# Five plain projection blocks, two pieces of fill per attention step, and more places for gates in a one-core decoder layer

## The chip, the cores and the metric

One core of a Trainium2 chip runs the whole layer in one program. The metric is device time in microseconds (us). TensorE does the matrix products into PSUM, VectorE (DVE in the profile) and ScalarE (ACT) read PSUM and SBUF, GpSimd (POOL) works on SBUF alone, and SyncE (SP) issues the DMAs.

## The reference, cut to what matters

The layer takes `x` (1024 tokens by 1024 channels). One projection `p = x @ w_in` feeds four token mixers: A, an RWKV-7 recurrence; B, a causal convolution; C, gated linear attention; D, forgetting attention (a causal softmax attention with a bias from cumulated log forget gates). Each mixer's output `u_b` (256 channels) is projected up to 1024 channels and gated:

```
gates  = sigmoid(p_gate.reshape(T, 4, D) + gate_b)
merged = gates[:, 0] * (u_rw @ rw_up)  + gates[:, 1] * (u_cv @ cv_up) \
       + gates[:, 2] * (u_gla @ gla_up) + gates[:, 3] * (u_fox @ fox_up)
x = layer_norm(ALPHA * x + merged @ w_out)
```

After that come a cross-attention and a SwiGLU network with their own residuals and norms. Everything is in float32.

## The kernel before, in words

A float32 product is made of three matmuls of a rounded type: each operand is split into a high part (a cast on ACT) and a low part (a subtraction, on DVE unless told otherwise) by `split` (lines 161 and 162), and `mm3` adds high*high, low*high and high*low (lines 179, 183, 182). A matmul has 512 columns, one half of the 1024 tokens.

**Projection (from line 407 on).** The weight matrix comes in blocks of 128 output columns. `plain(b)` makes one block: two halves of 8 x 3 matmuls, a copy out of PSUM on ACT, and `shift(b)`, the token shift in five DVE instructions (lines 327 to 331). Blocks 0, 1 and 8 are made so. The other blocks are made in pairs by `seven`, a Strassen-like scheme with 7 products of 4 x 3 matmuls in place of 8; it needs sums and differences of quarters of `x` and of the weights. `sums_of_x0(k)` makes those of `x`: four POOL instructions (`comb` at line 389, and line 449) and three splits into the tiles `xt`. It is called for k = 0 to 3, and each call sets one of the eight `xraw` places of the pool `pM` free, from which the plain blocks' results `praw` and the first weight `piece` take theirs. Block 8's weights (`w_misc`) are asked for just behind block 0.

**Mixers, with fill.** While the recurrence and the attentions run, TensorE's gaps are filled from a generator, `merge` (`pieces` at its call). A piece is six matmuls: a quarter of a half of a gate block (`gate_block`, tile `ps_g`; `ps_gate` for the first branch) or one product of `other_branches` (`ps_up`, a mixer output times `ups`). `weave(fill, streams, n)` draws n pieces and then takes one step of each stream. For forgetting attention n is `FOX_PIECES`, 3. `fox` has 20 steps for each of two head pairs, and `weave` draws once more at its end. `head` is one head and block of 128 queries, in three stages one step apart: scores (`ps_fs`, line 1094 for the mask), with maximum, exponential and normalisation on DVE and ACT; transposes (`ps_ft`, line 1115); output (`ps_fo`, line 1128, after every second one).

`merge` gives 80 pieces of the first branch, and then for j = 0 to 7 the 8 pieces of one of the last branch's gate blocks, followed by up to 4 products of the other branches, or up to 10 once forgetting attention has ended (`3 in ready`). The last branch, 3, can begin only then. `drain(pieces)` takes what is left.

A product of `other_branches` is six matmuls into one of two PSUM banks, a multiplication by the gate on DVE (line 1256), and an addition to `merged` on POOL (line 1257). The gates were stored in DRAM and come back by DMA into tiles `gsig` (line 1245); there are three places for them (tag `sg`), and `ahead` asks for them two products before their use. The outputs of a branch are loaded and split by `values` into `yh` and `yl`, which have room for one branch. After the products `merged` is split (`mA`, `mB`) and multiplied by `w_out`, whose weights take the places of `xh` and `xl` when the last gate block has been made.

**What sets the order.** Each engine's instructions are put in order by a planner at build time. It takes the first instruction in program order that is ready by its own cost estimates, and waits for a free place of the pool, so later work may move ahead of work that waits. On the chip the order of each engine is then fixed.

Of the kernel before, what the change touches and what calls it, by code (L numbers as in the profile page):

```python
# [11 lines left out]
F32 = mybir.dt.float32  # L12
# [4 lines left out]
ALU = mybir.AluOpType  # L17
PSUM = bass.MemoryType.PSUM
INVERSE = 14
FOX_PIECES = 3  # L20
DRAM = bass.MemoryType.DRAM

P = 128
# [3 lines left out]
TH = 512  # L27
# [10 lines left out]
ST_BLOCKS = ["cb0", "ca0", "cb1", "ca1", "gq", "gk", "gv0", "gv1", "gr0", "gr1",  # L38
             "fq0", "fk0", "fv0", "fq1", "fk1", "fv1"]
# [53 lines left out]
def hybrid_kernel(ctx, tc, io, out):  # L93
# [10 lines left out]
    pB = ctx.enter_context(tc.tile_pool(name="pB", bufs=9))  # L104
# [55 lines left out]
    def split(hi, lo, src, eng=nc.vector):  # L160
        nc.scalar.copy(hi, src)  # L161
        eng.tensor_tensor(out=lo, in0=src, in1=hi.bitcast(F32), op=ALU.subtract)  # L162

    def weight(src, pool=wp, th="whi", tl="wlo", eng=nc.vector, rp=wp, tr="raw"):
        raw = rp.tile([P, D], F32, tag=tr, name="wraw")
        nc.sync.dma_start(raw, src)
        hi = pool.tile([P, D], F32R, tag=th, name="whi")
        lo = pool.tile([P, D], F32R, tag=tl, name="wlo")
        split(hi, lo, raw, eng)
        return hi, lo  # L170
# [21 lines left out]
    def drain(gen, n=None):  # L192

        while n is None or n > 0:
            if next(gen, gen) is gen:
                return
            n = n if n is None else n - 1

    def collect(gen, res):
        res.append((yield from gen))  # L200
# [76 lines left out]
    def hs(hf):  # L277
        return slice(hf * TH, (hf + 1) * TH)
# [113 lines left out]
    def sums(raws):  # L392
        a11, a21, a22 = raws[0][:, 0:TH], raws[1][:, 0:TH], raws[1][:, TH:]
        s1 = comb(a21, a22, ALU.add)
        s2 = comb(s1, a11, ALU.subtract)
        return s1, s2, comb(a11, a21, ALU.subtract)

    def plain(bi, w=None, between=None):
        raw = pM.tile([P, T], F32, tag="M", name="praw")
        g = project(io["wblk"][bi], lambda hf, ps: nc.scalar.copy(raw[:, hs(hf)], ps), w)  # L400
        drain(g, 1)
        if between:
            between()
        drain(g)
        shift(bi, raw)

    with ExitStack() as es:
        xtp = es.enter_context(tc.tile_pool(name="xtp", bufs=12))
        pairs0 = list(range(2, 8, 2)) + list(range(9, 9 + len(ST_BLOCKS), 2))

        def rows(u):
            pool, tag = (pM, "M") if u % 2 else (wp, "raw")
            raws = []
            for i in range(2):
                raws.append(pool.tile([P, D], F32, tag=tag, name="wraw"))
                nc.sync.dma_start(raws[i], io["wblk"][pairs0[u] + i])
            return raws

        def making(sv):
            nxt, ss = rows(0), None  # L420
            for u in range(len(pairs0)):
                raws = nxt
                a = [r[:, i * TH:(i + 1) * TH] for r in raws for i in range(2)]
                s1, s2, s3 = ss or sums(raws)
                yield sv.piece(a[0])
                if u + 1 < len(pairs0):
                    nxt = rows(u + 1)
                for src in (a[1], s2, s1, s3, a[3]):
                    yield sv.piece(src)
                t = sv.piece(comb(a[1], s2, ALU.subtract))  # L430
                ss = sums(nxt) if u + 1 < len(pairs0) else None
                yield t

        sv = Sevens(((pM, "M"), (wp, "whi"), (wp, "wlo"), (wp, "whi"), (wp, "wlo")), making)
        plain(0, w_first)

        xt = [tuple([t[:, i] for t in ts for i in range(2)] for ts in
                    ([xtp.tile([P, 2, TH], F32R, tag="xt", name="xt") for _ in range(2)] for _ in range(2)))
              for _ in range(3)]

        def sums_of_x0(k):
            (b11, b12), (b21, b22) = ([xraw[i][:, hs(hf)] for hf in range(2)] for i in (k, k + HK))
            t1 = comb(b12, b11, ALU.subtract)
            split(xt[0][0][k], xt[0][1][k], t1)
            t2 = comb(b22, t1, ALU.subtract)
            split(xt[1][0][k], xt[1][1][k], t2)
            t3 = comb(b22, b12, ALU.subtract)
            split(xt[2][0][k], xt[2][1][k], t3)
            nc.gpsimd.tensor_tensor(out=b11, in0=b21, in1=t2, op=ALU.subtract)

        w_misc = weight(io["wblk"][8])
        for k in (0, 1):
            sums_of_x0(k)
        plain(1, w_second)
        for k in (2, 3):
            sums_of_x0(k)
        plain(8, w_misc, lambda: sv.top_up(3))

        def quarter(i, hf):
            return [t[:, hs(hf)] for t in xh[HK * i:HK * i + HK]], [t[:, hs(hf)] for t in xl[HK * i:HK * i + HK]]  # L460


        x12 = quarter(0, 1)
        for k in range(HK):
            split(x12[0][k], x12[1][k], xraw[k][:, hs(0)])
        rhs0 = (quarter(0, 0), quarter(1, 0), xt[1], xt[0], xt[2], x12, quarter(1, 1))

        def term():
            t = pM.tile([P, 2, TH], F32, tag="M", name="term")
            return t[:, 0], t[:, 1]  # L470

        def bank0():
            return gps("ps_g")

        for b in pairs0[0:3]:
            raws = [pM.tile([P, T], F32, tag="M", name="praw") for _ in range(2)]

            def done(i, l, a, ps):
                tt(out=raws[i][:, hs(l)], in0=a, in1=ps, op=ALU.add)

            sv.seven(rhs0, bank0, term, done)
            for i in range(2):
                shift(b + i, raws[i])
        for b in pairs0[3:]:
            held = {}

            def done(i, l, a, ps):
                n = BLOCKS[b + i]
                t = pM.tile([P, TH], F32, tag="M", name="stg2")
                tt(out=t, in0=a, in1=ps, op=ALU.add)  # L490
                if n[0] == "c":
                    if n[1] == "b":
                        act(t, t, AF.Sigmoid)
                    held.setdefault(l, []).append(t)
                    if len(held[l]) < 2:
                        return
                    tt(out=t, in0=t, in1=held[l][0], op=ALU.mult)
                    n = "cu" + n[2]
                elif n[:2] == "fq":
                    act(t, t, AF.Copy, scale=0.125)  # L500
                nc.sync.dma_start(st_d[n][:, hs(l)], t)

            sv.seven(rhs0, bank0, term, done)
        for k in range(HK):
            t = pM.tile([P, TH], F32, tag="M", name="x12")
            nc.sync.dma_start(t, io["xT"][k][:, hs(1)])
            split(x12[0][k], x12[1][k], t)
# [725 lines left out]
    def other_branches(t2):  # L1233

        for br in (1, 2, 3):
            while br not in ready:
                yield None
            y = values(br, t2)
            us, todo, sgs = [up_weights(br, 0, t2)], [(j, hf) for j in range(KD) for hf in range(2)], []

            def ahead(n):
                while len(sgs) < min(n, len(todo)):
                    j, hf = todo[len(sgs)]
                    t = t2.tile([P, TH], F32, tag="sg", name="gsig", bufs=3)
                    nc.sync.dma_start(t, gate_d[8 * br + j - 8, :, hs(hf)])
                    sgs.append(t)

            ahead(2)
            yield None
            for n, (j, hf) in enumerate(todo):  # L1250
                if hf == 0 and j + 1 < KD:
                    us.append(up_weights(br, j + 1, t2))
                pu = gps("ps_up", both=False)
                up_product(pu, us[j], y, hf)
                sg, mj = sgs[n], merged[j][:, hs(hf)]
                tt(out=sg, in0=sg, in1=pu, op=ALU.mult)  # L1256
                nc.gpsimd.tensor_tensor(out=mj, in0=mj, in1=sg, op=ALU.add)  # L1257
                ahead(n + 3)
                yield True

    def merge(t2):
# [14 lines left out]
    ready = {0}  # L1276
    with ExitStack() as es:
# [13 lines left out]
        with tc.tile_pool(name="t3", bufs=4) as t3:  # L1291
            c_d = []
            weave(pieces, [collect(fox_decay(t3, ps2), c_d)])
            weave(pieces, [fox(t3, ps2, c_d[0])], FOX_PIECES)
        drain(pieces)
# [459 lines left out]
    late = []  # L1755
# [101 lines left out]
    for k in range(HK):  # L1857
        t = diff(x2[k + HK][:, hs(0)], xt[0].h[k + HK].bitcast(F32))
# [78 lines left out]
    for n, sl in enumerate((slice(0, 512), slice(512, 768), slice(768, 1024))):  # L1937
        hf, w = sl.start // TH, sl.stop - sl.start
# [12 lines left out]
        ahead = 3 if n < 2 else 1  # L1951
# [110 lines left out]
```

## Time and profile before

| | |
|---|---|
| median of 3 runs | 2127.74 us (2120.87 to 2127.99) |
| profiled execution | 2121.39 us |
| its span, first to last instruction | 2119.6 us |
| TensorE busy | 2052.0 us (97%), 11392 matmuls |
| mean granted TensorE clock | 0.984 |

The profile is of one execution. In its rows a time is in us from the span's start, and "idle before" is the idle time of that engine ahead of the instruction, with what released it. A matmul's own time overlaps the next one's; the distance between two starts is what one costs.

### The profile page before, as it was taken

How to read it: one execution, taken by the hardware profiler on the slowest of the kernel's cores; microseconds unless marked ns; L12 is line 12 of the kernel's file. 1: busy time of each engine (PE TensorE's matmuls, PEld its weight loads, DVE VectorE, ACT ScalarE, POOL GpSimd, SP SyncE). 2: the span in 40 equal slices, each digit the busy share in tenths (PEclk: the TensorE clock that was granted, in tenths of full speed). 3: DMA queues.
4: the chain of work that ended last, by engine and by line, in shares of the span. 5: the costliest groups of instructions: out<-in, count | busy, mean ns of one | idle time of the engine just before them, and what ended most of it. 6: DMA issues, size and time to landing. Idle time of an engine off the chain costs nothing.

```text
span 2119.6 us, 29300 instructions
## 1 busy us (share of the span) xinstructions
PE 2052.0 (97%) x11392; PEld 1672.8 (79%) x11392; DVE 1305.0 (62%) x2249; ACT 782.4 (37%) x1332; POOL 437.0 (21%) x328
## 2 busy tenths in 40 slices
PE   8999999999999999997899999999999999999997
PEld 5888877877777787775689788877888888888877
DVE  8975465398624544545567445687566666666666
ACT  4332254222257465563134333344232222232331
POOL 5432200000000001214313100047121212222343
PEclk9999999999999999998999999999999999999998
DMA  5223343231222314336434212330311111211112
GB/s 168 70 79 110 105 132 91 68 99 62 75 99 83 89 44 139 106 104 192 136 115 127 75 38 65 105 120 22 118 40 40 66 54 41 70 50 40 54 47 80
DMA packets 100507, 181.09 MB, mean 85 GB/s; under 512 B 21030, under 2 KB 45400, under 8 KB 100368
## 3 DMA queue, kind: packets, MB, share of 16 engines
q1 hardware_dynamic: 100368, 179.21, 26.2%
q8 instruction: 90, 1.47, 0.3%
q14 instruction: 49, 0.40, 0.1%
HBM read 141.84 MB, written 37.34 MB: 85 GB/s over the span
## 4 chain that ended last, share of the span: by engine, by line
PE 84%; DVE 5%; POOL 3%; issue 3%; ACT 3%; DMA 2%; SPq 0%; DVEq 0%; POOLq 0%; ACTq 0%
PE ps_w L183 9%; PE ps_w L179 9%; PE ps_w L182 9%; PE ps_g L179 8%; PE ps_g L183 7%; PE ps_g L182 7%; PE ps_q L182 3%; PE ps_q L183 3%; PE ps_q L179 2%; PE ps_wo L182 1%; PE ps_wo L183 1%; PE ps_wo L179 1%; PE ps_gate L179 1%; PE ps_gate L183 1%; PE ps_gate L182 1%
## 5 line engine op out<-in xcount | busy, mean ns | idle before, releaser
L182 PE MATMUL ps_g<-xh,wlo 128*128 128x512 f32 x432 | 171.7, 397 | 4.1 <-DVE wlo L162 4.1
L183 PE MATMUL ps_g<-xl,whi 128*128 128x512 f32 x432 | 171.9, 398 | 0.0
L161 ACT CAST piece<-wraw 128x512 fp32r<-128x512 f32 x135 | 82.9, 621 | 202.6 <-PE ps_w L183 160.9
L179 PE MATMUL ps_g<-xh,whi 128*128 128x512 f32 x432 | 148.7, 418 | 0.8 <-ACT xh L161 0.8
L161 ACT CAST piece<-wcomb 128x512 fp32r<-128x512 f32 x116 | 70.7, 620 | 212.4 <-PE ps_w L183 133.2
L183 PE MATMUL ps_w<-hid,piece 128*128 128x512 f32 (+1 forms) x400 | 144.3, 368 | 2.4 <-DVE hid L162 2.4
L182 PE MATMUL ps_w<-hid,piece 128*128 128x512 f32 (+1 forms) x400 | 144.0, 367 | 0.0
L162 DVE TENSOR_TENSOR wlo<-wraw,whi 128x1024 fp32r<-128x1024 f32 x77 | 97.7, 1270 | 58.6 <-ACT whi L161 58.3
L389 POOL TENSOR_TENSOR wcomb<-wraw,wcomb 128x512 f32<-128x512 f32 x29 | 42.0, 1448 | 398.8 <-DVE piece L162 397.8
L1781 DVE TENSOR_TENSOR x<-x,ps_w 128x512 f32<-128x512 f32 x120 | 82.4, 687 | 65.4 <-PE ps_w L183 65.3
L162 DVE TENSOR_TENSOR piece<-wraw,piece 128x512 fp32r<-128x512 f32 x127 | 99.1, 783 | 34.8 <-ACT piece L161 31.7
L161 ACT CAST whi<-wraw 128x1024 fp32r<-128x1024 f32 x95 | 98.6, 1046 | 56.0 <-issue 18.4
L162 POOL TENSOR_TENSOR wlo<-wraw,whi 128x1024 fp32r<-128x1024 f32 x18 | 46.1, 2567 | 323.5 <-ACT whi L161 312.7
L183 PE MATMUL ps_w<-xT,piece 128*128 128x512 f32 x288 | 112.0, 389 | 0.0
L182 PE MATMUL ps_w<-xT,piece 128*128 128x512 f32 x288 | 112.0, 389 | 0.0
L179 PE MATMUL ps_w<-hid,piece 128*128 128x512 f32 (+1 forms) x400 | 108.8, 367 | 0.2 <-DVE x L1779 0.2
L389 POOL TENSOR_TENSOR wcomb<-wraw 128x512 f32<-128x512 f32 x60 | 82.6, 1377 | 99.9 <-DVE piece L162 50.3
L182 PEld LDWEIGHTS ps_g<-xh,wlo 128*128 128x128 f32 x432 | 82.3, 191 | 22.9 <-DVE wlo L162 4.6
L1257 POOL TENSOR_TENSOR merged<-merged,gsig 128x512 f32<-128x512 f32 x48 | 69.1, 1452 | 139.3 <-DVE gsig L1256 128.0
L183 PEld LDWEIGHTS ps_g<-xl,whi 128*128 128x128 f32 x432 | 82.4, 191 | 18.6 <-issue 0.8
L162 DVE TENSOR_TENSOR piece<-wcomb,piece 128x512 fp32r<-128x512 f32 x116 | 91.7, 798 | 6.3 <-ACT piece L161 5.6
L179 PEld LDWEIGHTS ps_g<-xh,whi 128*128 128x128 f32 x432 | 76.6, 192 | 22.4 <-issue 4.6
(528 smaller groups left out, 5304.4 us busy)
## 6 DMA issues: line engine op xcount, KB each, us to landing
wraw<-ffn_w SPq DMA_DIRECT2D x72, 512.0 KB, 5.5
wraw<-wblk SPq DMA_DIRECT2D x57, 512.0 KB, 3.6
gate_d<-gsig SPq DMA_DIRECT2D x48, 256.0 KB, 2.0
gsig<-gate_d SPq DMA_DIRECT2D x48, 256.0 KB, 2.9
wraw<-xa_wo SPq DMA_DIRECT2D x16, 512.0 KB, 3.5
xraw<-xT SPq DMA_DIRECT2D x16, 256.0 KB, 5.6
yld<-y_d SPq DMA_DIRECT2D x16, 256.0 KB, 2.6
uraw<-ups SPq DMA_DIRECT2D x32, 128.0 KB, 3.6
```

The costliest lines, as they stand in the source:

```text
L161: nc.scalar.copy(hi, src)
L162: eng.tensor_tensor(out=lo, in0=src, in1=hi.bitcast(F32), op=ALU.subtract)
L179: mm(ps, lhsT=pairs[i][0], rhs=pairs[i][2], start=start and i == 0, stop=False)
L182: mm(ps, lhsT=ll, rhs=rh, start=False, stop=False)
L183: latest[0] = mm(ps, lhsT=lh, rhs=rl, start=False, stop=stop and i == n + min(lag, n) - 1)
L389: nc.gpsimd.tensor_tensor(out=t, in0=a, in1=b, op=op)
L1257: nc.gpsimd.tensor_tensor(out=mj, in0=mj, in1=sg, op=ALU.add)
L1781: tt(out=xs, in0=xs, in1=ps, op=ALU.add)
```

## The change

The pair of blocks 2 and 3 leaves the seven-product scheme, and both are made by `plain`. The calls of `sums_of_x0` are spread: one ahead of each of blocks 1, 2, 3 and 8. `FOX_PIECES` goes from 3 to 2. Once forgetting attention has ended, the gates of `other_branches` take places of the pool `pB` (tag `B`, nine places, shared with attention's tiles before and with `mA` after) in place of the three of `sg`, and are asked for four products ahead in place of two.

```diff
-FOX_PIECES = 3
+FOX_PIECES = 2
...
-        pairs0 = list(range(2, 8, 2)) + list(range(9, 9 + len(ST_BLOCKS), 2))
+        pairs0 = list(range(4, 8, 2)) + list(range(9, 9 + len(ST_BLOCKS), 2))
...
-        w_misc = weight(io["wblk"][8])
-        for k in (0, 1):
-            sums_of_x0(k)
+        w = weight(io["wblk"][2])
+        sums_of_x0(0)
         plain(1, w_second)
-        for k in (2, 3):
-            sums_of_x0(k)
-        plain(8, w_misc, lambda: sv.top_up(3))
+        w, w_next = weight(io["wblk"][3]), w
+        sums_of_x0(1)
+        plain(2, w_next)
+        w, w_next = weight(io["wblk"][8]), w
+        sums_of_x0(2)
+        plain(3, w_next)
+        sums_of_x0(3)
+        plain(8, w, lambda: sv.top_up(3))
...
-        for b in pairs0[0:3]:
+        for b in pairs0[0:2]:
...
-        for b in pairs0[3:]:
+        for b in pairs0[2:]:
...
-                    t = t2.tile([P, TH], F32, tag="sg", name="gsig", bufs=3)
+                    late = 3 in ready
+                    t = (pB if late else t2).tile([P, TH], F32, tag="B" if late else "sg", name="gsig",
+                                                  bufs=9 if late else 3)
...
-                ahead(n + 3)
+                ahead(n + (5 if 3 in ready else 3))
```

## Rows read from the trace of the kernel before

**Rows 1.** The page: busy time by engine; TensorE in 40 slices, tenths.

```profile
PE 2052.0 (97%) x11392; PEld 1672.8 (79%) x11392; DVE 1305.0 (62%) x2249; ACT 782.4 (37%) x1332; POOL 437.0 (21%) x328
...
PE   8999999999999999997899999999999999999997
```

**Rows 2.** Waits of TensorE, 952.5 to 1031 us: total, times, longest.

```profile
PE ps_up L179 <- DVE gsig L1256: 12.0, 12, 2.0
PE ps_up L179 <- ACT yh L161: 8.2, 2, 6.7
PE ps_wo L179 <- ACT mA L161: 1.3, 1, 1.3
```

**Rows 3.** The same view, 19 to 62 us.

```profile
PE ps_g L182 <- DVE wlo L162: 4.1, 1, 4.1
PE ps_g L182 <- DVE piece L162: 3.2, 1, 3.2
PE ps_g L179 <- ACT piece L161: 1.4, 1, 1.4
```

**Rows 4.** Timeline of TensorE at the start: start, duration, count, idle before.

```profile
23.95 0.39 PE L182 MATMUL ps_g<-xh,wlo 128*128 128x512 f32 x1
24.18 0.39 PE L183 MATMUL ps_g<-xl,whi 128*128 128x512 f32 x1
...
35.06 0.80 PE L182 MATMUL ps_g<-xh,wlo 128*128 128x512 f32 x1 [4.14 <-DVE wlo L162]
...
40.72 0.39 PE L183 MATMUL ps_g<-xl,whi 128*128 128x512 f32 x1
...
47.77 0.39 PE L183 MATMUL ps_g<-xl,whi 128*128 128x512 f32 x1
...
60.23 1.07 PE L179 MATMUL ps_g<-xt,piece 128*128 128x512 f32 x4
```

**Rows 5.** Timeline of VectorE and GpSimd in the same stretch.

```profile
30.05 1.60 POOL L449 TENSOR_TENSOR xraw<-xraw,wcomb 128x512 f32<-128x512 f32 x1
...
32.12 1.75 DVE L331 SCALAR_TENSOR_TENSOR r<-r,par,praw 128x512 f32<-128x512 f32 x1
33.79 1.21 DVE L162 TENSOR_TENSOR wlo<-wraw,whi 128x1024 fp32r<-128x1024 f32 x1
...
59.09 0.68 DVE L329 TENSOR_TENSOR misc<-praw 128x512 f32<-128x512 f32 x1
```

**Rows 6.** By stretch: busy us of PE, PEld, DVE, ACT, POOL; granted clock; DMA.

```profile
727.00:952.40 225.40, 222.29 (x1289) 177.80 (x1287) 108.93 (x243) 139.71 (x246) 31.44 (x24) 1.00 0.29 94
```

**Rows 7.** The same view: `ps_up`'s instructions alone (PE, PEld, DVE), then `ps_g`'s.

```profile
952.40:1028.00 75.60, 45.30 (x168) 32.81 (x168) 18.12 (x27) 0.91 0.57 181
...
952.40:1028.00 75.60, 9.81 (x42) 7.80 (x42) 0.00 (x0) 1.38 (x2) 0.91 0.57 181
```

**Rows 8.** Timeline of the last branch's products on VectorE and GpSimd.

```profile
1016.49 2.73 POOL L1257 TENSOR_TENSOR merged<-merged,gsig 128x512 f32<-128x512 f32 x2 [1.29 <-DVE gsig L1256]
...
1016.95 0.69 DVE L1256 TENSOR_TENSOR gsig<-gsig,ps_up 128x512 f32<-128x512 f32 x1 [0.60 <-DMA gsig<-gate_d]
1017.55 0.52 DVE L162 TENSOR_TENSOR ul<-uraw,uh 128x256 fp32r<-128x256 f32 x1
1018.47 1.30 DVE L162 TENSOR_TENSOR mA<-merged,mA 128x512 fp32r<-128x512 f32 x1 [0.40 <-ACT mA L161]
```

**Rows 9.** Timeline of one attention unit, from its masked scores to the normalisation.

```profile
783.61 0.23 PE L1094 MATMUL ps_fs<-lvl,identb 128*128 128x128 bf16 x1
...
784.93 1.28 ACT L1104 ACT_TABLE_LOAD   x1 [1.48 <-DVE fst L1101]
...
786.22 0.69 ACT L1104 ACTIVATE fp<-ps_fs,fst 128x512 f32<-128x512 f32 x1
...
787.88 0.62 DVE L1108 TENSOR_SCALAR fp<-fp,fst 128x768 f32<-128x768 f32 x1
...
787.94 1.31 PE L1128 MATMUL ps_fo<-fpt,fvr 128*64 128x128 f32 x20
```

## The prediction
> **What bounds the kernel now.** The page's first two parts come first: TensorE is busy 97% of the span and near 9 tenths in nearly every slice, so only two things can move the time, the number of matmuls and the few places where TensorE stands still [rows 1]. On the change's path the slices show two such places: the first slice, and the nineteenth and twentieth, where the granted clock is low as well, 0.91 over the tail [rows 7]. The waits of TensorE, asked for these stretches alone, name them. Near the middle it waits 12.0 us in 12 waits for the gate's multiplication, 8.2 us for a new branch's values and 1.3 us for the split of `merged`; this is the tail behind forgetting attention [rows 2]. At the start it waits once for the low part of a weight block and then twice for the first weight pieces of the seven-product pairs, 8.7 us in all [rows 3]. Every other stretch on the change's path is dense: in the attention stage TensorE is busy 222.29 of 225.40 us at full clock [rows 6]. So I price the change as matmuls added, plus stalls removed, plus stalls made.
>
> The price of a matmul of 512 columns is the distance of two starts, 24.18 - 23.95 = 0.23 us; over dense runs of twelve it is 2.72 us, so 0.2266 each [rows 4]. [...]
>
> **Five plain blocks.** Removed: one pair, 7 x 12 = 84 matmuls. Added: two plain blocks, 2 x 48 = 96. Net 12 x 0.2266 = 2.7 us more.
>
> What it buys is cover. In the kernel before, the last plain block ends at 47.77 + 0.23 = 48.0 us, and the third product starts at 60.23. Between lie 24 matmuls, worth 5.4 us; 12.2 - 5.4 = 6.8 us are lost to the two waits for pieces and to the low clock behind them [rows 3, 4]. VectorE is what is late: it does shifts, sums and pieces in one line, and its two-operand instructions take 1.75 us while GpSimd makes sums (1.60 us each), against 0.68 alone [rows 5]. The change puts 96 matmuls, 21.8 us, between block 8's old place and the first pair. VectorE's own extra work there is two shifts (the four long instructions of each) and two low parts: 2 x (4 x 0.68 + 1.21) = 8 us alone, 2 x (4 x 1.75 + 1.21) = 16 us if GpSimd runs beside all of it [rows 5]. GpSimd gets nothing more before the first pair, so it ends earlier against that work. Even 16 is under 21.8, so I take the 6.8 us as gone. If the new low parts of blocks 3 and 8 come late themselves, each costs at most what the one in the trace does, 4.1 + 2.7 = 6.8 us.
>
> [...]
>
> The other wait stays. The 4.1 us at 35.06 is for the low part of the third block, at 33.79, which VectorE does only when block 0's shift has ended [rows 3 to 5]. In the change block 2's weights are asked for at exactly that place in the order, behind the same shift, with the same first sums on GpSimd. The bounds are 6.8 us won if it goes, and nothing. I take nothing. Sum of this part: 2.7 - 6.8 = -4.1 us, between -10.9 (both stalls go) and +9.5 (the pieces' stall goes, both new low parts late).
>
> **Two pieces a step.** Forgetting attention has 40 steps and `weave` draws once more, so the stage consumes 41 x 3 = 123 pieces, and 82 after. 41 pieces of 6 matmuls, 41 x 6 x 0.2266 = 55.7 us, move behind it. By itself this is worth nothing on a full engine. It matters for what is left to lay into the tail. Before, the tail holds 42 matmuls of gate blocks and 168 of products [rows 7]: 210 x 0.2266 = 47.6 us of work in 75.6 us. 28.0 us are lost, waits and low clock together. In that tail all gate blocks are over after the first 9.8 us, and what follows is products alone, each waiting for its gate.
>
> After, 76 pieces are left. Going through `merge` with 82: 46 pieces of the first branch (123 less 57 gate pieces and 20 products done by then), gate blocks 0 to 2 and half of 3, and 8 products. The tail holds the other half of block 3, four whole blocks, and 40 products; it runs block by block, 8 gate pieces (10.9 us) and then at most 10 products. The two changes of branch then fall ahead of a gate block: values are loaded and split while 10.9 us of matmuls run, against 8.2 us of wait before [rows 2].
>
> **More places for gates.** Why a product costs 2.0 us before (GpSimd takes 1.29 + 2.73 = 4.02 us for two, waiting included): a gate's place is set free by GpSimd's addition, reloaded, and VectorE waits for the DMA, 0.60 us in the row [rows 8]. With three places the loop of load, multiplication and addition sets the pace. With nine and four ahead it doesn't. Next late is VectorE in the last branch: two multiplications 2 x 0.69, `ul` 0.52 and `mA` 1.30 make 3.2 us for two products, against 2.72 of matmuls and 2.73 of GpSimd [rows 8]. So 16 products lose 8 x 0.5 = 4 us; the upper bound is the old pace, 16 x (2.01 - 1.36) = 10, and the lower 0, since the last gate block can be drawn into these gaps. I take 4. I add 1 us for changes of branch (bounds 0 and 8.2, the wait seen). `w_out`'s weights can now be split only when the last gate block is done, six products or 8.2 us ahead of their use, where before they had the whole tail. The nearest row is a low part, 1.21 us, and the cast and load ahead of it; I take 1 us, bounds 0 and 6.8 (the whole stall that a late weight cost at the start). The 1.3 us for the last split stays.
>
> **What the attention steps lose.** Fewer pieces stand between a unit's scores and its transposes. In the trace the mask matmul starts at 783.61 and the normalisation ends at 788.50: 4.9 us, 1.28 of it a table load, paid where a gate's sigmoid came between; without it 3.6 [rows 9]. TensorE covered it with 3 pieces (4.08 us) and `ps_fo` (1.31). With two it has 2.72, `ps_fo` on every second step, and what the planner draws ahead: the next unit's scores or more fill, since neither depends on this unit. If it draws ahead rightly the loss is 0. If it draws nothing, a long unit (16 of 32) lacks 4.3 - 2.7 - 0.6 = 1.0 us on average, a short one little, so some 16 us, and twice that where the stops bring the low clock. I take 4 us, near the end that the trace shows: 3.1 us of idle in 225 [rows 6].
>
> [...]
>
> **Sum.** Tail and attention: -28.0 + 4 + 1 + 1 + 4 = -18.0 us. With the start, -22.1 us. The profiled execution took 2121.39 us (span 2119.6 and 1.8 around it): 2099.3 us. The median of the three runs shown is 6.3 us above that execution, which lies near their low end, so I put 2101.
>
> **Rivals.**
> *Everything goes (10%).* The first wait goes too (-6.8) and attention and tail lose nothing (-10): 2083 to 2090 us. For it: the attention stage is nearly dense before. Against: block 2's low part stands where block 8's did.
> *The tail stays bound by its chains (20%).* Gate blocks run as blocks and the products at some 1.75 us all the same: 40 x 0.4 = 16 us in place of 6, and attention loses 6 in place of 4: 2101 + 12 = 2113 us, up to 2119 with a late `w_out`. For it: GpSimd's 2.73 us for two leave no slack. Against: no place is waited for any more.
> *A new low part comes late (10%).* Block 8's low part can be made only when block 2 has set its place free, at about 48 us, and stands behind block 2's shift. At 1.75 us an instruction that is 48 + 4 x 1.75 + 1.21 = 56 us and a cast before it, against block 3's end at 59 [rows 4, 5]. Two splits of `xt` ahead of it in the order and TensorE stops again: 6.8 us, 2108 us. Against: GpSimd has ended the sums by then, and alone the shift takes 3 us.
> *Attention becomes the bound, and the kernel slower (8%).* A unit's chain, 3.6 to 4.9 us, is longer than two pieces. If the order fixed at build time puts the transposes right behind the fill, all 32 units wait, the long ones about 2 us and the short ones 1, and stops of that length bring the low clock, as the tail's 0.91 shows [rows 2, 7]. 16 x 2 + 16 x 1 = 48 us in place of 4: 2101 + 44 = 2145 us, and 2128 where every second unit is covered. From (22 + 4)/32 = 0.8 us a unit on, all that the rest saves is used up. Against: work that is ready may be drawn ahead, and the stage has next to no waits before.
> *No effect (4%).* The gates' places collide with `mA`'s in the same pool, and both new low parts come late: 2117 to 2127 us.
> The forecast holds 48%: 2094 to 2108 us.
>
> **How the numbers follow.** Half a per cent, 10.6 us, is about what a measurement of this kernel can tell from no change: against 2127.74, faster means below 2117. Forecast, first and third rival, 68%, are faster, and half of the second: 0.78. The rest of the second, the last and a little of the fourth are within it: 0.15. Slower than 2138: 0.07. The range takes the forecast, the third rival, most of the second and half of the first: 2086 to 2120.
>
> **What would show it.** Right: TensorE's waits at the start hold the 4.1 us for `wlo` and none for `piece`; the time from the first plain block to the third product is 15 us longer (21.8 - 6.8); the attention stage is 50 to 56 us shorter with few waits for `fp`; products in the tail follow at 1.4 to 1.7 us between gate blocks; the clock in the tail is near 1.00; 11404 matmuls. Wrong: waits of `ps_ft` for `fp` over 10 us; new waits for `wlo` near 48 or 59 us; waits of `ps_wo` for `whi`; an attention stage shortened by less than 45 us.

## The result, and the profile after

The changed kernel takes **2096.74 us**, median of 4 runs (2095.68 to 2100.91), against 2127.26 us for the kernel before beside it. The ratio is 0.9867, with a 95% interval of 0.9843 to 0.9890: by this ratio 28 us, or 1.3%, faster. The profiled execution took 2095.68 us, where the one before took 2121.39, so the two profiles differ by 25.7 us. The forecast worked from the profiled execution came to 2099.3.

First the busy lines and the slices of the page:

```profile
PE 2050.9 (98%) x11404; PEld 1673.4 (80%) x11404; DVE 1292.9 (62%) x2237; ACT 768.0 (37%) x1320; POOL 431.9 (21%) x324
...
PE   8999999999999999999999999999999999999997
...
PEclk9999999999999999999999999999999999999998
```

There are 12 matmuls more, as counted, and TensorE is busy 1.1 us less: before, part of its busy time was matmuls at a low clock (0.91 granted over the tail [rows 7]). The dip in slices 19 and 20 [rows 1] is gone. Next the stretches: forgetting attention, then the tail behind it up to the last product of a branch, and the waits of TensorE in the tail:

```profile
724.70:897.80 173.10, 170.57 (x1047) 133.77 (x1045) 90.88 (x217) 113.00 (x215) 14.86 (x12) 1.00 0.25 78
897.80:1004.50 106.70, 104.27 (x452) 84.09 (x453) 56.99 (x74) 28.58 (x49) 55.92 (x39) 1.00 0.55 179
```

```profile
PE ps_up L179 <- DVE gsig L1263: 2.4, 2, 1.6
```

Attention is 51.8 us shorter (225.40 us in [rows 6], at slightly other marks). The tail is longer, since the fill that attention no longer consumes is in it, but it is dense: one kind of wait, 2.4 us, is left of 20.2 [rows 2], and the granted clock is 1.00 where it was 0.91 [rows 7]. The waits at the start, 15 to 100 us:

```profile
PE ps_g L182 <- DVE wlo L162: 2.7, 1, 2.7
```

Both waits for `piece` [rows 3] are gone, and the one for `wlo` is still there. The third product:

```profile
75.05 1.07 PE L179 MATMUL ps_g<-xt,piece 128*128 128x512 f32 x4
```

The gain by step, from the two profiles (us). The marks are the last `ps_fo`, `ps_up` and `ps_wo` and the first `ps_fs`:

| stretch | before | after | difference |
|---|---|---|---|
| up to attention | 727.6 | 724.7 | -2.9 |
| forgetting attention | 224.9 | 173.1 | -51.8 |
| tail: gate blocks and products | 75.0 | 106.7 | +31.7 |
| `w_out` | 106.0 | 104.2 | -1.8 |
| the rest | 986.1 | 985.2 | -0.9 |

40 pieces, 40 x 6 x 0.2266 = 54.4 us, have gone from the second row to the third. So attention lost 2.6 us by having less fill, and the tail won 22.7 us: it stood still or ran slowly for 27.4 us before and for 4.7 after. The rest holds the same work in all the kernels of this document and took 985.2 to 989.1 us in their profiles; a difference of a few us there says nothing about an edit.

### The profile page after: what moved, and what is told of

Read it like the earlier page. It is cut to its first block, busy times and chain, and to the rows that moved or that the text cites. A ratio compares the mean times of both kernels' runs of the same rounds, so it can differ in the third digit from the quotient of the medians.

```text
span 2093.9 us, 29285 instructions
## 1 busy us (share of the span) xinstructions
PE 2050.9 (98%) x11404; PEld 1673.4 (80%) x11404; DVE 1292.9 (62%) x2237; ACT 768.0 (37%) x1320; POOL 431.9 (21%) x324
## 4 chain that ended last, share of the span: by engine, by line
PE 88%; DVE 3%; POOL 3%; DMA 2%; ACT 2%; issue 2%; SPq 0%; DVEq 0%; POOLq 0%; ACTq 0%
PE ps_w L183 9%; PE ps_w L182 9%; PE ps_w L179 9%; PE ps_g L179 8%; PE ps_g L183 8%; PE ps_g L182 8%; PE ps_q L182 3%; PE ps_q L183 3%; PE ps_q L179 2%; PE ps_gate L179 1%; PE ps_wo L182 1%; PE ps_wo L183 1%; PE ps_wo L179 1%; PE ps_gate L183 1%; PE ps_up L179 1%
## 5 line engine op out<-in xcount | busy, mean ns | idle before, releaser
L182 PE MATMUL ps_g<-xh,wlo 128*128 128x512 f32 x464 | 184.5, 398 | 2.7 <-DVE wlo L162 2.7
L183 PE MATMUL ps_g<-xl,whi 128*128 128x512 f32 x464 | 184.9, 398 | 0.0
L179 PE MATMUL ps_g<-xh,whi 128*128 128x512 f32 x464 | 160.1, 417 | 2.2 <-ACT xh L161 2.2
L182 PEld LDWEIGHTS ps_g<-xh,wlo 128*128 128x128 f32 x464 | 88.6, 191 | 22.7 <-DVE wlo L162 3.1
L183 PEld LDWEIGHTS ps_g<-xl,whi 128*128 128x128 f32 x464 | 88.7, 191 | 19.8 <-issue 0.8
L179 PEld LDWEIGHTS ps_g<-xh,whi 128*128 128x128 f32 x464 | 83.4, 192 | 25.9 <-ACT xh L161 4.7
L389 POOL TENSOR_TENSOR wcomb<-wraw 128x512 f32<-128x512 f32 x58 | 78.4, 1352 | 101.2 <-DMA wraw<-ffn_w 46.8
L162 DVE TENSOR_TENSOR piece<-wcomb,piece 128x512 fp32r<-128x512 f32 x112 | 87.3, 786 | 11.0 <-ACT piece L161 10.4
```

The source lines that it names most:

```text
L179: mm(ps, lhsT=pairs[i][0], rhs=pairs[i][2], start=start and i == 0, stop=False)
L182: mm(ps, lhsT=ll, rhs=rh, start=False, stop=False)
L183: latest[0] = mm(ps, lhsT=lh, rhs=rl, start=False, stop=stop and i == n + min(lag, n) - 1)
L389: nc.gpsimd.tensor_tensor(out=t, in0=a, in1=b, op=op)
```

## Experiments

**The three parts, each alone on the kernel before.** The theory priced each part by what it removes; the rival is that they need each other.

Of the change's diff, `plain_only` has the hunks on `pairs0`, `plain` and `sums_of_x0`; `fox_only` has the line `FOX_PIECES = 2`; `places_only` has the last two hunks, on the tile `gsig` and on `ahead`.

> The kernel before with the five plain blocks alone. Theory: the pieces' stall at the start goes (6.8 us) for 12 matmuls more (2.7 us), so 3 to 4 us faster than before; the wait for the third block's low part stays at 3 to 4 us, the attention stage at 225 us and the tail behind it at 76 us. Rival (new low parts of blocks 3 and 8 come late): one more wait for wlo near 48 or 59 us, and 2 to 10 us slower.

> The kernel before with two pieces of fill a step alone, three places for gates. Theory (fill and places both count): the attention stage is some 52 us shorter as in the changed kernel, branch changes are covered by gate blocks, but products still wait for their gates at about 2.0 us each; 8 to 14 us faster than before, waits of ps_up for the gate 8 us or more. Rival (the fill alone does it): gate pieces are drawn into the products' waits, 20 us or more faster, waits of ps_up under 4 us.

> The kernel before with nine places for gates, asked for four products ahead, alone. Theory: the products of the tail go from 2.0 to about 1.65 us, VectorE being next, and the change of branch still waits 7 us or more for its values; 8 to 12 us faster than before. Rival (the places alone do it): 18 us or more faster. Other rival (places don't matter, the additions on GpSimd set the pace): within 3 us of before.

Measured: `plain_only` 2119.85 us, ratio 0.9977 (0.9966 to 0.9988); `fox_only` 2120.19, 0.9977 (0.9968 to 0.9987); `places_only` 2119.40, 0.9970 (0.9961 to 0.9980). The first came out about as expected (its wait for the third block's low part was 1.5 us, not 3 to 4, and 1.1 us of wait for a `piece` was left). The other two won less than the theory said. By these ratios the parts win 4.9, 4.9 and 6.4 us, each give or take some 2, 16 together, where the whole wins 28. TensorE's waits in the tail of `fox_only`, and then in that of `places_only`, show what each leaves:

```profile
PE ps_up L179 <- DVE gsig L1256: 10.8, 11, 1.8
PE ps_g L179 <- DVE gsig L1256: 1.2, 2, 0.9
```

```profile
PE ps_up L179 <- DVE gsig L1258: 6.8, 6, 1.8
PE ps_up L179 <- ACT yh L161: 5.4, 2, 4.4
```

With two pieces alone, the changes of branch (`yh`, 8.2 us in [rows 2]) cost nothing any more, because gate blocks run meanwhile; but the products behind each gate block wait for gates as before. With the places alone, it is the other way about: VectorE never waits for a gate's DMA in this tail (8 times, 7.4 us, in that of the kernel before), but the 28 products run back to back and the changes of branch stay bare. What TensorE waits for now stands in the orders of VectorE and ScalarE:

```profile
967.46 1.92 DVE L162 TENSOR_TENSOR wlo<-wraw,whi 128x1024 fp32r<-128x1024 f32 x1 [0.53 <-ACT whi L161]
969.31 0.67 DVE L1258 TENSOR_TENSOR gsig<-gsig,ps_up 128x512 f32<-128x512 f32 x1
970.04 0.72 PE L179 MATMUL ps_up<-yh,uh 128*128 128x512 f32 x2 [1.16 <-DVE gsig L1258]
...
992.46 1.05 ACT L161 CAST whi<-wraw 128x1024 fp32r<-128x1024 f32 x1 [4.51 <-DMA wraw<-w_out]
993.41 0.61 ACT L161 CAST yh<-yld 128x512 fp32r<-128x512 f32 x1
994.08 0.79 PE L179 MATMUL ps_up<-yh,uh 128*128 128x512 f32 x1 [4.36 <-ACT yh L161]
```

Once the last gate block is made, `w_out`'s weights are loaded and split. Their low parts stand on VectorE ahead of the products' multiplications, and their casts on ScalarE ahead of the next branch's values, one of them waiting 4.51 us for its DMA. Of the 12.2 us of waits, 10.1 end right behind such a split (four for the gate, 4.7 us, and both for `yh`), and the last 2.1 behind a split of `merged`. The stop of 4.36 us lies in a stretch at a granted clock of 0.56:

```profile
990.00:1000.00 10.00, 5.92 (x17) 4.72 (x18) 5.56 (x8) 2.59 (x4) 2.24 (x3) 0.56 0.73 240
```

**The change without the places.** This separates "the parts add up" from "the places pay only together with the fill".

```diff
-                    late = 3 in ready
-                    t = (pB if late else t2).tile([P, TH], F32, tag="B" if late else "sg", name="gsig",
-                                                  bufs=9 if late else 3)
+                    t = t2.tile([P, TH], F32, tag="sg", name="gsig", bufs=3)
...
-                ahead(n + (5 if 3 in ready else 3))
+                ahead(n + 3)
```

> The changed kernel with the old three places, asked for two products ahead: the other two parts together. Theory: as fox_only with 3 to 4 us of the start on top, 11 to 18 us faster than before, 12 to 18 us slower than the changed kernel. Rival (the fill alone does it): within 5 us of the changed kernel.

Measured: 2114.73 us, ratio 0.9954 (0.9935 to 0.9972), 18.0 us slower than the change and, by the ratio, 9.8 us faster than before, a little less than the 11 to 18 expected. Plain blocks and two pieces add up to within the interval (0.23% + 0.23% against 0.46%). So the places win 6.4 us on the kernel before and 18 us on top of the other two: the excess over the sum is between the places and these two together. That it is the fill, and not the plain blocks, is read from the tails and was not run. In the tail of `no_places` a few products follow at the pace of matmuls, 1.37 to 1.53 us, and then TensorE waits:

```profile
957.07 0.62 PE L179 MATMUL ps_up<-yh,uh 128*128 128x512 f32 x2
...
958.44 0.74 PE L179 MATMUL ps_up<-yh,uh 128*128 128x512 f32 x2
...
959.97 0.71 PE L179 MATMUL ps_up<-yh,uh 128*128 128x512 f32 x2
...
963.35 0.73 PE L179 MATMUL ps_up<-yh,uh 128*128 128x512 f32 x2 [1.74 <-DVE gsig L1261]
```

VectorE's waits in this tail name what was late, the gate's DMA; the change has no such wait there:

```profile
DVE gsig L1261 <- DMA gsig<-gate_d: 12.7, 11, 2.8
```

**The gate blocks first, the products after.** The places and the two pieces are kept, but in the tail no product is laid between gate blocks. Theory: interleaving hides the changes of branch and lets GpSimd and VectorE catch up. Rival: places alone make the products dense.

```diff
-            for _ in range(10 if 3 in ready else 4):
+            for _ in range(0 if 3 in ready else 4):
```

> The changed kernel, but once forgetting attention has ended all gate blocks that are left are made first, and the 40 products follow in one run (0 in place of 10 products behind each block). Nine places for gates and two pieces a step stay. Theory (gate blocks between the products are half of the gain: they give GpSimd and VectorE time and cover the changes of branch): products at 1.55 to 1.65 us each as in places_only, 8 to 11 us lost, and some 8 us of waits for yh; 14 to 22 us slower than the changed kernel. Rival (the places alone keep the products dense once there is enough of them): within 5 us of the changed kernel.

Measured: 2123.14 us, ratio 0.9994 (0.9982 to 1.0006): 26 us slower than the change, more than the theory asked for, and nothing is left of the gain. TensorE's waits in its tail:

```profile
PE ps_up L179 <- ACT yh L161: 9.5, 3, 4.8
PE ps_up L179 <- DVE gsig L1263: 6.7, 7, 1.6
```

The longest of them, and what stood ahead of it on ScalarE; then a stretch of 5 us with `w_out`'s splits over, and GpSimd's additions from 974.96 us on:

```profile
966.86 1.05 ACT L161 CAST whi<-wraw 128x1024 fp32r<-128x1024 f32 x1 [4.62 <-DMA wraw<-w_out]
967.82 1.14 ACT L161 CAST yh<-yld 128x512 fp32r<-128x512 f32 x2
968.48 0.80 PE L179 MATMUL ps_up<-yh,uh 128*128 128x512 f32 x1 [4.82 <-ACT yh L161]
...
980.00:985.00 5.00, 5.00 (x24) 4.13 (x23) 3.25 (x7) 0.67 (x2) 5.00 (x5) 1.00 0.81 235
...
974.96 18.72 POOL L1264 TENSOR_TENSOR merged<-merged,gsig 128x512 f32<-128x512 f32 x14 [1.82 <-DVE gsig L1263]
```

The theory got the loss, but only half of its reason. GpSimd needs no gate blocks to catch up: fourteen additions in a row took 1.34 us each, and TensorE stayed full beside them, as the rival had it. What stops the products is, again, `w_out`: 9.8 of the 16.2 us of waits end right behind one of its splits, 4.3 stand at the last change of branch, whose values come late from DMA, and 2.1 behind a split of `merged`. So the gate blocks between the products do two things in the change: they run while a branch's values come in, and, the last of them being late, they keep `w_out`'s splits out of the way until six products are left. What each is worth no run separates; it would take one with the gate blocks first and `w_out`'s splits held back.

The tails side by side, by the stretches and the waits as above. Work is 210 or 450 matmuls at 0.2266 us; what is lost beyond the waits is matmuls that start late by less than the profile calls a wait, or run at a low clock (0.91, 0.92 and 0.93 granted over the tails of the first, the second and the fifth row):

| kernel | tail | work | lost | of it waits |
|---|---|---|---|---|
| before | 75.0 | 47.6 | 27.4 | 20.2 |
| places only | 65.7 | 47.6 | 18.1 | 12.2 |
| two pieces only | 120.6 | 102.0 | 18.6 | 12.0 |
| plain and two pieces | 120.8 | 102.0 | 18.8 | 11.9 |
| gate blocks first | 127.4 | 102.0 | 25.4 | 16.2 |
| the change | 106.7 | 102.0 | 4.7 | 2.4 |

**How many places, and how far ahead.** The forecast had a loop of load, multiplication and addition that three places can't cover. `four_places` holds five of the nine places with idle tiles until the last branch's thirteenth product; `two_ahead` keeps nine places and asks as late as the kernel before.

```diff
 four_places:
+HELD = 5
...
+        held = []
...
+                    if late and not held:
+                        for _ in range(HELD):
+                            held.append(pB.tile([P, TH], F32, tag="B", name="held"))
+                            nc.gpsimd.memset(held[-1][:, 0:8], 0.0)
...
+                if br == 3 and n == 12:
+                    for h in held:
+                        nc.gpsimd.memset(h[:, 0:8], 0.0)
 two_ahead:
-                ahead(n + (5 if 3 in ready else 3))
+                ahead(n + 3)
```

> The changed kernel with five of the nine places for gates held by idle tiles until the last branch's thirteenth product, so that four are left. Theory (a place goes round in 3 x 2.01 = 6.0 us): 1.5 us a product inside a run of products against 1.36 with enough places, 2 to 7 us slower than the changed kernel and 10 us or more faster than with three. Rival (it is not the number of places but that these lie in another pool or are asked for earlier): within 1.5 us of the changed kernel.

> The changed kernel with nine places, but the gates asked for two products ahead, as before. Theory (the planner issues a load as soon as there is a place, wherever it is asked for): no change, within 3 us of the changed kernel. Rival (the distance sets when a load goes out): products at 1.7 us or more, 8 us or more slower.

Measured: 2096.33 us, ratio 0.9871 (0.9853 to 0.9888), and 2096.88, 0.9866 (0.9845 to 0.9887): both as the change. `two_ahead` came out by its theory, `four_places` at the sign of its rival. I had put the loop at 6.0 us, which four places would not hide at 1.36 us a product; the tail with four is 104.60 us, as dense as with nine:

```profile
896.90:1001.50 104.60, 104.31 (x454) 84.11 (x453) 55.68 (x74) 28.49 (x48) 56.74 (x38) 1.00 0.56 182
```

So the loop, in this mix, is at most 4 x 1.36 = 5.4 us. Three places cover 4.1 us of products, and with them VectorE waited for the DMA eleven times in `no_places`; with four it never does. How far ahead the program asks does nothing, since the planner's order came out the same on every engine. That it is the fourth place, and not the other pool that the places lie in, was not run: no kernel has three places in `pB`. The tail of `two_ahead`, the change's order once more, took 105.4 us where the change's took 106.7, so a microsecond or two between tails means nothing.

**One piece a step.** Is attention near its own bound at two? (Six products at most, in place of ten, stand behind a gate block, so that the last branch finds its gates made.)

```diff
-FOX_PIECES = 2
+FOX_PIECES = 1
-            for _ in range(10 if 3 in ready else 4):
+            for _ in range(6 if 3 in ready else 4):
```

> The changed kernel with one piece of fill a step (and at most 6 products behind a gate block in place of 10, so that the last branch finds its gates made). Theory (a unit's chain of 3.6 to 4.9 us is longer than one piece, but the planner draws fill ahead): the attention stage shrinks by 35 to 50 us, less than the 55.7 us moved, waits of ps_ft for fp and of ps_fs rise above 8 us, and the kernel is 5 to 20 us slower than the changed one. Rival (fill is drawn ahead so well that the number doesn't matter): the stage shrinks by 52 us or more, time within 4 us of the changed kernel.

Measured: 2128.47 us, ratio 1.0018 (1.0007 to 1.0028), 32 us slower than the change. Its attention stage:

```profile
725.70:875.30 149.60, 142.13 (x872) 106.94 (x870) 77.11 (x202) 87.04 (x187) 4.23 (x4) 0.97 0.13 41
```

```profile
PE ps_ft L1120 <- DVE fp L1113: 2.7, 5, 1.0
PE ps_fo L1133 <- ACT fpt L1121: 1.7, 5, 0.5
```

175 matmul records have left it (1047 against 872), 39.7 us of work, and it got 23.5 us shorter: 16 us are lost. The waits seen there are for a unit's chain, 7.1 us with two smaller ones beside those shown, against 2.4 in the change; the granted clock of 0.97 and small delays make the rest. A step now takes 149.6 / 40 = 3.74 us, inside the 3.6 to 4.9 us worked out for the chain from [rows 9]. Most of the other half is lost behind it: the tail takes 157.9 us for 104 pieces, 141.4 us of work, 16.5 lost against 4.7. The theory had the direction and missed the sizes: less left the stage than the 55.7 us it counted with, the waits of `ps_ft` and `ps_fs` came to 4.0 us, not over 8, and the kernel lost 32 us, not 5 to 20. The mechanism of the rival "attention becomes the bound" is real; at two pieces it had cost 2.6 us.

**The wait at the start.** The forecast left the wait for `wlo` of the third block in place. `early_low_part` asks for that block's weights ahead of the first plain block.

```diff
         sv = Sevens(...)
+        w = weight(io["wblk"][2])
         plain(0, w_first)
...
-        w = weight(io["wblk"][2])
         sums_of_x0(0)
```

> The changed kernel with block 2's weights asked for ahead of block 0's product in place of behind it, so that VectorE makes their low part before block 0's token shift. Theory (the third block waits only because that low part stands behind the shift): the wait for wlo goes from 2.7 to under 0.7 us and the low clock behind it goes too, the third product of the first pair comes 4 to 6 us earlier than the changed kernel's 75.0 us, 2091 to 2093 us. Rival (the next thing is late there: PSUM banks of the plain blocks, or block 3's low part): a wait of 2 us or more in another place before 75 us, and less than 2 us won.

Measured: 2099.03 us, ratio 0.9884 (0.9869 to 0.9900): nothing won, and the sign of the rival: the wait moved, by TensorE's waits at the start and ScalarE's timeline:

```profile
PE ps_g L179 <- ACT whi L161: 3.2, 1, 3.2
```

```profile
55.69 0.62 ACT L161 CAST xt<-wcomb 128x512 fp32r<-128x512 f32 x1 [2.74 <-POOL wcomb L389]
56.22 0.58 ACT L400 COPY praw<-ps_g 128x512 f32<-128x512 f32 x1
56.70 1.05 ACT L161 CAST whi<-wraw 128x1024 fp32r<-128x1024 f32 x1
```

Block 8's weights are late now: their cast stands on ScalarE behind a cast of `xt` that waits 2.74 us for GpSimd's sum. In the change the same cast ran at 54.76, while TensorE still had matmuls of the block before, and cost nothing. This is the third rival's place, reached by another engine. VectorE's early low part cost more as well:

```profile
27.95 1.74 POOL L389 TENSOR_TENSOR wcomb<-xraw 128x512 f32<-128x512 f32 x1
28.46 2.31 DVE L162 TENSOR_TENSOR wlo<-wraw,whi 128x1024 fp32r<-128x1024 f32 x1
```

2.31 us, against 1.21 in [rows 5]: 1.23 of them lie beside a sum of GpSimd's, under way until 29.69, and 1.08 behind it.

`early_two` repairs it: the last two groups of sums are issued behind the split of block 8's weights (`made_by` holds the two instructions of the last split).

```diff
         w, w_next = weight(io["wblk"][8]), w
-        sums_of_x0(2)
+        act_i, dve_i = (m.ins for m in made_by)
+        with tc.issue_after(act_i), tc.issue_after(dve_i):
+            sums_of_x0(2)
+            sums_of_x0(3)
         plain(3, w_next)
-        sums_of_x0(3)
```

> early_low_part, and besides block 8's weights are split before ScalarE and VectorE may begin the last two groups of sums (k = 2 and 3). Theory (with the third block's wait gone, the fifth waits because the cast of its weights stands behind casts that wait for GpSimd's sums): no wait of ps_g for whi or wlo before the first pair, the third product 3 to 6 us earlier than in early_low_part (77.3 us, its first matmul 0.5 us late), 2090 to 2094 us. Rival (the sums themselves are what is late, the work of VectorE and GpSimd sets the start): the wait turns up at the first pair, for xt or a piece, and the third product is within 2 us of 77.

Measured: 2095.12 us (2093.86 to 2096.20), ratio 0.9859 (0.9842 to 0.9876). In its place the theory held; the time stayed above the 2090 to 2094 expected. TensorE's waits from 5 to 100 us:

```profile
PE ps_g L181 <- ACT xh L161: 1.5, 3, 0.8
PE ps_g L184 <- DVE piece L162: 0.3, 1, 0.3
```

```profile
71.12 1.07 PE L181 MATMUL ps_g<-xt,piece 128*128 128x512 f32 x4
```

No wait for `wlo` or `whi`; the third product starts at 71.1 us, 3.9 us before the change's 75.0 and 6.2 before that of `early_low_part`. Its median beats both kernels', but its interval overlaps that of the change, so that it is the faster one is not shown. At the end of `w_out` its profile is 4.1 us ahead; 2.2 of them came back in the rest, 987.4 us against 985.2, which is within the 985.2 to 989.1 that the same work takes.

## Why the prediction was right, point by point

**Start: forecast -4.1 us, measured -2.9 between the two profiles.** The third product came 14.8 us later (60.2 to 75.0), and 15.0 were forecast. The remaining 1.2 us lie within what equal starts differ by: the stage behind the projection began at 609.3, 612.3 and 611.7 us in the three kernels with the old start, and at 605.2 to 607.4 in seven with the new one (mean 606.1, so -5.0 against the mean of the old). `plain_only`'s 4.9 us by its ratio says the same. The wait for `wlo` stayed, as forecast, between 1.5 and 4.4 us in those seven; a wait for `piece`, 1.1 us, was left in `plain_only` alone. "Both new low parts late" didn't happen; the shift among which block 8's stands ran at 0.69 to 0.75 us an instruction, not at 1.75, and the low part took its 1.22:

```profile
55.02 0.69 DVE L329 TENSOR_TENSOR k<-praw 128x512 f32<-128x512 f32 x1
55.74 0.75 DVE L331 SCALAR_TENSOR_TENSOR k<-k,par,praw 128x512 f32<-128x512 f32 x1
56.40 1.22 DVE L162 TENSOR_TENSOR wlo<-wraw,whi 128x1024 fp32r<-128x1024 f32 x1
```

The 6.8 us that the bounds and the rivals set for a late low part are the wait of 4.1 us before it and 2.7 for a low clock behind that wait. In the kernel before, the 13 matmuls behind it took 5.66 us, 0.435 each against 0.2266, at a granted clock of 0.51; in the change the 14 behind its wait of 2.7 us took 4.89 at 0.65, 1.7 more than 14 x 0.2266:

```profile
35.06:40.72 5.66, 5.66 (x13) 4.47 (x14) 5.66 (x6) 1.64 (x3) 4.88 (x4) 0.51 0.32 93
...
35.88:40.77 4.89, 4.89 (x14) 3.90 (x15) 4.89 (x7) 2.48 (x4) 1.66 (x1) 0.65 0.37 109
```

**Attention: forecast a loss of 4 us, measured 2.6.** The waits of `ps_ft` for `fp` are 2.4 us in all, far from the 10 that would have spoken against it:

```profile
PE ps_ft L1120 <- DVE fp L1113: 2.4, 4, 0.9
```

The planner had drawn work of the next unit ahead: the scores that end at 771.1 us have 16 matmuls of fill and, from 774.6, the next unit's seven score matmuls in front of their transposes at 776.2. That this hangs by little is shown by `one_piece`.

**Tail: forecast 28.0 won and 5 lost again, measured 27.4 and 4.7; `w_out`: forecast 1 lost, measured 1.8 won.** The order was as worked out (half a gate block, then four whole ones with at most ten products behind each), with 75 pieces for 76. The terms inside were mis-sized, and that they add up is partly luck. 4 us were set for VectorE in the last branch, for `ul` and the split of `merged` beside the multiplications. But the splits of `merged` came only at the very end (on VectorE from 1002.67 us on), and the branch's first ten products, from 969.23 to 982.83, lost nothing. Its last six lost 2.2 us, nearly all in one wait behind a low part of `w_out`, where TensorE put one matmul of `w_out` into the gap:

```profile
1000.00 2.15 DVE L162 TENSOR_TENSOR wlo<-wraw,whi 128x1024 fp32r<-128x1024 f32 x1 [0.75 <-ACT whi L161]
1000.86 0.40 PE L179 MATMUL ps_wo<-mA,whi 128*128 128x512 f32 x1
1002.08 0.68 DVE L1263 TENSOR_TENSOR gsig<-gsig,ps_up 128x512 f32<-128x512 f32 x1
1002.80 0.73 PE L179 MATMUL ps_up<-yh,uh 128*128 128x512 f32 x2 [1.55 <-DVE gsig L1263]
```

So the price of late `w_out` weights was paid here, among the products, and not at `w_out`: there the 1 us set for it wasn't paid, and the 1.3 us for `mA` that I had left standing went; that stretch is 1.8 us shorter and TensorE has no wait in it. The other wait of the tail, 0.9 us, is in the branch before. The 1 us for changes of branch was not paid: there is no wait for `yh`.

**What failed is a thought behind the sum, not the sum.** I gave the tail's 28 us to three causes as if each edit removed its own: the places the pace of 2.0 us, the fill the changes of branch. The expectations for `fox_only` and `places_only` were written from that, and both missed. In the tail either edit alone wins about 9 us (27.4 to 18.6 and to 18.1), and the change wins 22.7, 4.6 more than the two. As much again lies at `w_out`: `places_only` takes 108.8 us there, 2.8 more than before, with a wait of 2.5 for `mA`, while the change wins 1.8. And the sum, which knew that `w_out`'s splits had the whole tail before, gave them no price among the products; in `places_only` and `gates_first` most of the waits that are left stand behind them.

**The rivals.** The tail stays bound by its chains: it does in `no_places` (18.8 us lost) and in `gates_first` (25.4), so the rival was one place or one ordering away. A new low part late: seen in `early_low_part` alone, 3.2 us. Attention as the bound: seen at one piece, not at two. This rival, like the doubled bound for the attention steps, also had stops of 1 to 2 us bring the low clock, from the tail's mean of 0.91. The rows of the kernel before don't bear that out for stops of 1 us: the clock is 0.51 around the stop of 6.7 us for `yh`, and 1.00 where TensorE stops for 1.0 us every 4.

```profile
990.00:1000.00 10.00, 3.35 (x8) 2.67 (x9) 5.56 (x7) 2.28 (x3) 1.40 (x1) 0.51 0.72 241
1010.00:1020.00 10.00, 7.41 (x31) 5.21 (x29) 7.89 (x11) 2.86 (x6) 6.64 (x5) 1.00 0.50 157
```

## What to carry to other kernels

Where two engines make a chain per unit of work and TensorE has other work that depends on none of it, lay that work between the units rather than ahead of them: the same instructions in another order were worth 26 us here. See what that order does to the work of the next stage as well: part of these 26 us stood behind `w_out`'s splits, which lay ahead of the products in one order and mostly behind them in the other. Count the places of a ring that a DMA fills before its distance: four were as good as nine, and an earlier request did nothing. Try the parts of a change alone before their gains are added, and look at what stands ahead in each engine's order when something is made earlier.

## What was not expected of the hardware

Around a stop of TensorE for a change of branch, the granted clock was 0.56 over 10 us in `places_only`. Over the tails it is 0.91 before, 0.92 in `places_only` and 0.93 in `gates_first`, and 1.00 in the other three of the table. In those three the 6.6, 6.9 and 2.3 us that are lost on top of the visible waits are therefore small delays alone. In the first three, 5.9 to 9.2 us are lost on top, part of it to the low clock; how much was not separated.
